# A decoder layer's output projection as seven products of 2x2 blocks, with W's block sums made by accumulating DMA

## The chip, the cores and the metric

One core of a Trainium2 chip runs the whole program. The metric is the device time of one execution in microseconds (us). Most executions of this kernel agree within 0.3%.

## The reference

The input x has 512 rows of 1024 channels. The layer computes h = RMSNorm(x) and one wide projection of h, which gives q, k, v and a gate path z for two attention branches (8 heads of 64 each) and two merge gates. Branch a is block-sparse softmax attention with a relative bias, branch b is stick-breaking attention. The end of the layer, where the change lies, is:

```python
ya = (merge_heads(oa) * jax.nn.silu(za)) @ w_up_moba[l]        # 512x512 @ 512x1024
yb = (merge_heads(ob) * jax.nn.silu(zb)) @ w_up_sb[l]
y = jax.nn.sigmoid(gl_a + gb[:D_MODEL]) * ya + jax.nn.sigmoid(gl_b + gb[D_MODEL:]) * yb
x = x + y @ w_out[l]                                            # 512x1024 @ 1024x1024
```

All of it is float32.

## The kernel before

**Precision.** Every large product is made of three matmuls of the float32r type (`mm3`, lines 144 to 147): each operand is split into a high part (a ScalarE copy that rounds) and a low part (VectorE subtracts the high part), and high x low, low x high and high x high are added in PSUM.

**Weights.** The host lays all weights out as chunks of 128 x 1024 in the order of use. `load_w` keeps three chunks ahead: `fetch_w` loads a chunk into a `wr` buffer (line 98, SyncE's queue, SP), ScalarE makes `wh` (line 107) and VectorE `wl` (line 109). There are three buffers of each.

**Order of the work.** The four projections qa, ka, va, vb come first. Then a loop over eight pairs of heads (four of branch a, four of branch b): the scores of both heads (six PSUM banks with the tag "s"), for each head softmax or stick-breaking, a transpose on VectorE (`turned`), a store to DRAM and a load back (`put`, `get`), the split of P (`split_p`), and `finish` for the pair before it: the product with V (`po`, line 418, one "s" bank) and its gate. Between these steps the list `FILLS` puts other projections, one chunk each, that keep TensorE (PE) fed: z, the merge gates g:0 to g:15, q and k of branch b, and `up("a", c)`. Each takes a bank with the tag "pj", of which there are two. Entry 4m + 2 of the list is the one between the two `finish` calls of pair m (26 is g:9, 30 is g:12). `up(br, c)` makes two tiles of y: PE sums the four blocks of 128 channels of one branch into a "pj" bank, VectorE multiplies it with the gate (line 476) and, for branch b, adds branch a's part (478) and splits y into `yh` (481) and `yl` (482). After the loop come `up("b", 0)` to `up("b", 3)`, then the output projection: for each half m of the columns, four row tiles of 128, eight k blocks, four chunks of W, each chunk used by 24 matmuls; the last row tile of the second half is cut into two of 256 columns. VectorE adds x to each bank (line 559) and SP stores it (560).

A scheduler in the compiler fixes the order of each engine's queue. It takes what it holds to be ready, earliest in the program first, so an instruction can stand in the queue ahead of others that come before it in the program. Buffers are handed out from pools by tag; an instruction that takes a buffer waits until the last reader of its former tenant is done.

Of the kernel before, what the change touches and what calls it, by code (L numbers as in the profile page):

```python
# [10 lines left out]
F32 = mybir.dt.float32  # L11
F32R = mybir.dt.float32r
BF16 = mybir.dt.bfloat16
AF = mybir.ActivationFunctionType
ALU = mybir.AluOpType
AX = mybir.AxisListType

P = 128
S = 512
D = 1024  # L20
KT = D // P
NT = S // P
H = 8
# [4 lines left out]
BIG = 1e30  # L28
TW = S + P
SM = 32  # L30
WARM = 8
BLK = [0, 4, 7, 9, 10]
PQ = BLK[-1] * 32


FILLS = ("za:0", "za:1", "za:2", "",
# [11 lines left out]
def hybrid_layer(ctx: ExitStack, tc: tile.TileContext, x, xT, w, rel, out):  # L48
    nc = tc.nc
    V, A, G, T = nc.vector, nc.scalar, nc.gpsimd, nc.tensor  # L50
# [3 lines left out]
    wp = ctx.enter_context(tc.tile_pool(name="wp", bufs=3))  # L54
    xp = ctx.enter_context(tc.tile_pool(name="xp", bufs=8))
    vp = ctx.enter_context(tc.tile_pool(name="vp", bufs=8))
# [7 lines left out]
    def bank(tag, name):  # L64
        return pp.tile([P, S], F32, tag=tag, bufs=BANKS[tag], name=name)

    def slot(name, dt=F32):
        return gp.tile([P, S], dt, tag="g", name=name)


    warm = tp.tile([P, S], BF16, tag="sx", bufs=2, name="warm")
    V.memset(warm, 0.0)
    half = cp.tile([P, NT], F32, name="half")
    G.memset(half, -0.5)
    spare = cp.tile([P, NT], F32, name="spare")
    A.activation(spare, half, AF.Copy)
    x0 = cp.tile([P, SM + S], F32, name="x0")
    sm = x0[:, :SM]
    nw, mb, qw, kw = sm[:, 0:8], sm[:, 8:24], sm[:, 24:25], sm[:, 25:26]


    ahead, low = [], {}
    count = [0]

    def load_w():

        while len(ahead) < 3 and count[0] < w.shape[0]:
            ahead.append(fetch_w(count[0]))
            count[0] += 1
        return ahead.pop(0)  # L90

    def fetch_w(c):
        raw = wp.tile([P, 1024], F32, tag="wr", bufs=3, name=f"wr{c}")
        cuts = ((0, 512), (512, 1024)) if c == 0 else ((0, 1024),)
        for a, b in cuts:
            if 0 < c < 4:
                raw_x(2 * c)
            nc.sync.dma_start(raw[:, a:b], w[c][:, a:b])
            if a == 0 and c < 4:
                for k in (0, 1) if c == 0 else (2 * c + 1,):  # L100
                    raw_x(k)
        hi = wp.tile([P, 1024], F32R, tag="wh", name=f"wh{c}")
        lo = wp.tile([P, 1024], F32R, tag="wl", name=f"wl{c}")
        if c == 0:
            low[c] = load_x(0)
        for a, b in cuts:
            A.activation(hi[:, a:b], raw[:, a:b], AF.Copy)  # L107
            with tc.issue_after(low[0]) if c == 0 else nullcontext():
                low[c] = V.tensor_tensor(lo[:, a:b], raw[:, a:b], hi[:, a:b].bitcast(F32), op=ALU.subtract).ins  # L109
        return hi, lo  # L110
# [6 lines left out]
    def raw_x(k):  # L117
        if k == 0:
            xraw[k] = x0[:, SM:]
            nc.sync.dma_start(x0, xT[:, :SM + S])  # L120
        else:
            xraw[k] = slot(f"xr{k}")
            nc.sync.dma_start(xraw[k], xT[:, SM + k * S:SM + (k + 1) * S])
# [17 lines left out]

    GROUPS = (("pj", "pj", "s", "s"), ("s", "s", "s", "s"))

    def mm3(ps, aH, aL, bH, bL, start, stop):
        T.matmul(ps, aH, bL, start=start, stop=False)  # L145
        T.matmul(ps, aL, bH, start=False, stop=False)  # L146
        T.matmul(ps, aH, bH, start=False, stop=stop)  # L147

    def section_tc(group, name, first=False, hooks=None):
        ps = [bank(GROUPS[group][t], f"{name}{t}") for t in range(NT)]  # L150
# [24 lines left out]
    def steps(c, n=NT):  # L175

        if c == 3:
            return [(kk, i) for i in range(n) for kk in range(2)]
        return [(kk, i) for kk in range(2) for i in range(n)]
# [3 lines left out]
    r = cp.tile([P, NT], F32, name="r")  # L183

    def row_norm():
# [5 lines left out]
        G.tensor_tensor(r, ss[:, 0, :], ss[:, 1, :], op=ALU.add)  # L191
        G.tensor_scalar(r, r, 1.0 / D, EPS, op0=ALU.mult, op1=ALU.add)
        G.tensor_tensor(r, r, half, op=ALU.pow)
# [98 lines left out]
    st, rows, last, qa, ka = {}, {}, {}, [], []  # L292
# [29 lines left out]
    v_of["b"] = split_v(ps_vb, "vb", [1.0] * NT)  # L322


    def chunk_ct(name):
        hi, lo = load_w()
        ps = bank("pj", name)
        for k in range(KT):
            ks = slice(k * P, (k + 1) * P)
            mm3(ps, hi[:, ks], lo[:, ks], xH[k], xL[k], k == 0, k == KT - 1)  # L330
        return ps
# [58 lines left out]
    def put(br, h):  # L390
        dr = dp.tile([P, 4 * PQ], F32, tag="pd", bufs=4, name=f"pd{br}{h}")
        for a in range(4):
            nc.sync.dma_start(bass.AP(tensor=dr.tensor, offset=dr.offset + a * PQ,
                                      ap=[[4 * PQ, 32], [32 * 4 * PQ, 4], [1, PQ]]),
                              turned[a * 32:(a + 1) * 32].rearrange("c q k r -> c q (k r)"))
        return dr

    def get(br, h, dr):
        pt = tp.tile([P, 4 * PQ], F32R, tag="pt", bufs=3, name=f"pt{br}{h}")
        nc.scalar.dma_start(pt.bitcast(F32), dr)  # L400
        return pt

    def split_p(br, h, pt):
        hi = tp.tile([P, 4 * PQ], F32R, tag="th", bufs=2, name=f"th{br}{h}")
        A.activation(hi, pt.bitcast(F32), AF.Copy)  # L405
# [37 lines left out]
    gates = {}  # L443
# [19 lines left out]


    yH, yL = [], []

    def up(br, c):
        hi, lo = load_w()
        for u in range(2):
            n = 2 * c + u  # L470
            ps = bank("pj", f"y{br}{n}")
            for p in range(4):
                ks = slice((u * 4 + p) * P, (u * 4 + p + 1) * P)
                mm3(ps, hi[:, ks], lo[:, ks], oH[br, p], oL[br, p], p == 0, p == 3)
            g = gates[n if br == "a" else 8 + n]
            V.tensor_tensor(g, ps, g, op=ALU.mult)  # L476
            if br == "b":
                V.tensor_tensor(g, g, gates[n], op=ALU.add)
                h = xp.tile([P, S], F32R, tag="xh", name=f"yh{n}")
                l = xp.tile([P, S], F32R, tag="xl", name=f"yl{n}")  # L480
                A.activation(h, g, AF.Copy)
                V.tensor_tensor(l, g, h.bitcast(F32), op=ALU.subtract)
                yH.append(h)
                yL.append(l)


    make = {"za": lambda i: f_z("a", i), "zb": lambda i: f_z("b", i), "q": f_q, "k": f_k, "g": f_g,
            "up": lambda i: up("a", i)}
    fills = [[(kind, int(i)) for kind, i in (word.split(":") for word in part.split())] for part in FILLS]

    def fill():
        for kind, i in fills.pop(0):
            make[kind](i)

# [14 lines left out]
    for m, (br, p) in enumerate(PAIRS):  # L509
        q, k = (qa, ka) if br == "a" else (qb, kb)  # L510
        sc, rw = {h: [None] * NT for h in (2 * p, 2 * p + 1)}, {h: [None] * NT for h in (2 * p, 2 * p + 1)}
        scores(br, p, q, k, sc)
        for b in range(2):
            h = 2 * p + b
            bias = load_bias(h) if br == "a" else None
            (softmax if br == "a" else stick)(h, sc[h], rw[h], bias, (3, 2, 1, 0))
            turn(br, h, rw[h])
            done[m, b] = put(br, h)
            fill()
            if not b:  # L520
                done[m, 0] = get(*head(m, 0), done[m, 0])
        for b in range(2):
            if m:
                finish(m - 1, b)
            if not b:
                done[m, 1] = get(*head(m, 1), done[m, 1])
            done[m, b] = split_p(*head(m, b), done[m, b])
            fill()
    fill()
    finish(len(PAIRS) - 1, 0)  # L530
    fill()
    finish(len(PAIRS) - 1, 1)
    fill()
    assert not fills

    for c in range(4):
        up("b", c)

    for m in range(2):
        ms = slice(m * S, (m + 1) * S)  # L540
        res = []
        for t in range(NT):
            xr = slot(f"xres{m}{t}")
            nc.sync.dma_start(xr, x[t * P:(t + 1) * P, ms])
            res.append(xr)
        parts = [(t, 0, S) for t in range(NT)]
        if m == 1:
            parts[3:] = [(3, 0, S // 2), (3, S // 2, S)]
        ps = [bank((GROUPS[1 - m] + ("s",))[i], f"out{m}{i}") for i in range(len(parts))]
        for c in range(4):  # L550
            hi, lo = load_w()
            for kk, i in steps(c, len(parts)):
                t, a, b = parts[i]
                k = 2 * c + kk
                ts = slice(t * P, (t + 1) * P)
                cs = slice(kk * S + a, kk * S + b)
                mm3(ps[i][:, :b - a], yH[k][:, ts], yL[k][:, ts], hi[:, cs], lo[:, cs], k == 0, k == KT - 1)
        for i, (t, a, b) in enumerate(parts):
            V.tensor_tensor(res[t][:, a:b], ps[i][:, :b - a], res[t][:, a:b], op=ALU.add)
            nc.sync.dma_start(out[t * P:(t + 1) * P, m * S + a:m * S + b], res[t][:, a:b])  # L560


def _t5_runs():
# [67 lines left out]
```

## Time and profile before

| | |
|---|---|
| median of 3 runs | 406.7 us (406.35 to 407.4) |
| the profiled execution | 407.05 us, of which the profile's span is 405.2 us |
| PE (matmuls) busy | 396.9 us, 98% of the span |
| VectorE (DVE) busy | 287.7 us, 71% |
| ScalarE (ACT) busy | 213.4 us, 53% |
| GpSimd (POOL) busy | 33.9 us, 8% |

Times in the rows are counted in us from the span's start. A row of a group of instructions names the line, engine, operation, written and read tiles, the shape and the count, and behind the bar the busy time, the mean duration of one in ns, and the idle time of the engine before them with what ended it. In a timeline the first two numbers are start and duration; brackets hold the idle time before the instruction and what ended it. Matmuls overlap, so their price is read from start to start.

### The profile page before, as it was taken

What the parts mean: (1) busy time and instruction counts of PE and PEld (TensorE: products, weight loads), DVE (VectorE), ACT (ScalarE), POOL (GpSimd) and SP (SyncE); (2) the same over time, 40 slices, a digit from 0 to 9 for tenths busy, and PEclk for the clock granted to TensorE, in tenths of its full rate; (3) what the DMA queues carried; (4) which work ended last, traced back from release to release, by engine and by line L of the source; (5) the groups of instructions that cost most, each with busy time, mean ns of one, the idle gap of its engine ahead of it and who ended that gap; (6) DMA issues with size and microseconds to landing.
All of it is one profiled execution on the core that took longest, in us unless ns stands there. A gap on an engine that the chain in (4) does not pass through costs nothing.

```text
span 405.2 us, 5404 instructions
## 1 busy us (share of the span) xinstructions
PE 396.9 (98%) x1920; PEld 328.0 (81%) x1920; DVE 287.7 (71%) x524; ACT 213.4 (53%) x353; POOL 33.9 (8%) x76
## 2 busy tenths in 40 slices
PE   8999999999999999999999999998998999999996
PEld 4788888887888888888888888886887888888885
DVE  4832759939788786888799599698589456862412
ACT  4772144646777879696763663563392454331110
POOL 2029953000000000000000000000000000000000
PEclk9999999999999999999999999999999999999999
DMA  8954277141677675756528537537526547433202
GB/s 264 356 212 133 79 235 258 66 142 52 171 220 222 213 237 167 213 180 228 175 68 246 171 104 231 172 97 228 168 80 194 163 135 246 146 105 104 104 2 104
DMA packets 28283, 67.77 MB, mean 167 GB/s; under 512 B 3288, under 2 KB 11736, under 8 KB 28256
## 3 DMA queue, kind: packets, MB, share of 16 engines
q1 hardware_dynamic: 24800, 54.84, 42.8%
q10 hardware_dynamic: 3456, 12.58, 9.8%
q8 instruction: 15, 0.25, 0.2%
q14 instruction: 12, 0.10, 0.1%
HBM read 54.81 MB, written 12.61 MB: 166 GB/s over the span
## 4 chain that ended last, share of the span: by engine, by line
PE 87%; DVE 5%; DMA 3%; ACT 2%; issue 1%; SPq 1%; DVEq 0%; ACTq 0%
PE gl L145 7%; PE gl L147 6%; PE gl L146 6%; PE out L146 4%; PE out L145 4%; PE out L147 4%; PE poa L418 2%; PE sa L345 2%; DVE sx L373 2%; PE za L145 2%; PE kb L145 2%; PE zb L145 2%; PE qb L145 2%; PE kb L147 2%; PE qb L147 2%; PE vb L147 2%
## 5 line engine op out<-in xcount | busy, mean ns | idle before, releaser
L109 DVE TENSOR_TENSOR wl<-wr,wh 128x1024 fp32r<-128x1024 f32 (+1 forms) x65 | 78.5, 1208 | 51.4 <-ACT wh L107 51.1
L107 ACT ACTIVATE wh<-wr 128x1024 fp32r<-128x1024 f32 (+1 forms) x65 | 67.8, 1043 | 60.6 <-PE out L147 20.5
L145 PE MATMUL gl<-xl,wh 128*128 128x512 f32 x128 | 51.0, 398 | 3.1 <-DVE gl L476 3.1
L146 PE MATMUL gl<-xh,wl 128*128 128x512 f32 x128 | 49.9, 390 | 0.0
L147 PE MATMUL gl<-xh,wh 128*128 128x512 f32 x128 | 49.9, 390 | 0.0
L145 PEld LDWEIGHTS gl<-xl,wh 128*128 128x128 f32 x128 | 24.0, 188 | 8.3 <-DVE gl L476 3.4
L147 PEld LDWEIGHTS gl<-xh,wh 128*128 128x128 f32 x128 | 24.0, 188 | 5.2
L146 PEld LDWEIGHTS gl<-xh,wl 128*128 128x128 f32 x128 | 24.1, 188 | 4.6
L146 PE MATMUL out<-wh,yl 128*128 128x512 f32 (+1 forms) x72 | 26.4, 366 | 0.0
L145 PE MATMUL out<-wl,yh 128*128 128x512 f32 (+1 forms) x72 | 26.4, 366 | 0.0
L147 PE MATMUL out<-wh,yh 128*128 128x512 f32 (+1 forms) x72 | 26.3, 365 | 0.0
L373 DVE TENSOR_TENSOR_SCAN sx<-om,begin 128x512 f32<-128x512 f32 (+3 forms) x32 | 24.6, 807 | 0.7 <-ACT om L369 0.7
L357 ACT ACTIVATE pa<-pa,m 128x512 f32<-128x512 f32 (+3 forms) x32 | 17.8, 558 | 6.4 <-DVE m L355 5.9
L405 ACT ACTIVATE thb<-ptb 128x1280 fp32r<-128x1280 f32 x8 | 10.2, 1273 | 15.2 <-DMA ptb<-pdb 15.2
L369 ACT ACTIVATE om<-sb 128x512 f32<-128x512 f32 (+3 forms) x32 | 14.8, 469 | 3.0 <-DVE sx L373 3.0
L448 ACT ACTIVATE gl<-gl,x 128x512 f32<-128x512 f32 x16 | 11.1, 695 | 9.9 <-PE gl L147 9.7
L406 DVE TENSOR_TENSOR ptb<-ptb,thb 128x1280 fp32r<-128x1280 f32 x8 | 11.9, 1482 | 5.7 <-ACT thb L405 5.7
L145 PEld LDWEIGHTS out<-wl,yh 128*128 128x128 f32 x72 | 13.6, 189 | 2.3
L147 PEld LDWEIGHTS out<-wh,yh 128*128 128x128 f32 x72 | 13.6, 188 | 2.2
L146 PEld LDWEIGHTS out<-wh,yl 128*128 128x128 f32 x72 | 13.6, 189 | 2.2
L355 DVE CUSTOM_DVE_ANT_0 pa<-sa,om 128x512 f32<-128x512 f32 (+3 forms) x32 | 14.9, 477 | 0.4 <-PE sa L345 0.3
L387 DVE STREAM_TRANSPOSE turned<-pa 128x256 f32<-128x256 f32 (+1 forms) x48 | 15.1, 367 | 0.0
(239 smaller groups left out, 975.5 us busy)
## 6 DMA issues: line engine op xcount, KB each, us to landing
wr<-in_w SPq DMA_DIRECT2D x63, 512.0 KB, 4.3
pda<-turned SPq DMA_DIRECT2D x32, 160.0 KB, 2.9
pta<-pda ACTq DMA_DIRECT2D x8, 640.0 KB, 3.9
pdb<-turned SPq DMA_DIRECT2D x32, 160.0 KB, 2.9
ptb<-pdb ACTq DMA_DIRECT2D x8, 640.0 KB, 3.9
xn<-in_x SPq DMA_DIRECT2D x8, 256.0 KB, 4.8
xs<-in_xT ACTq DMA_DIRECT2D x8, 256.0 KB, 3.1
om<-e_dr SPq DMA_DIRECT2D x8, 256.0 KB, 3.8
```

Of the source, the lines that this page charges most:

```text
L107: A.activation(hi[:, a:b], raw[:, a:b], AF.Copy)
L109: low[c] = V.tensor_tensor(lo[:, a:b], raw[:, a:b], hi[:, a:b].bitcast(F32), op=ALU.subtract).ins
L145: T.matmul(ps, aH, bL, start=start, stop=False)
L146: T.matmul(ps, aL, bH, start=False, stop=False)
L147: T.matmul(ps, aH, bH, start=False, stop=stop)
L355: V.tensor_tensor_reduce(p, sc[i], bias[:, S - n:], scale=1.0, scalar=3e38, op0=ALU.add, op1=ALU.min, accum_out=m[:, 0:1])
L357: A.activation(p, p, AF.Exp, bias=m[:, 0:1], scale=-1.0, accum_out=m[:, 1:2])
L369: A.activation(om[:, e - 1 - n:e - 1], z, AF.Sigmoid, scale=-1.0)
L373: V.tensor_tensor_scan(sx[:, n - 1::-1] if n == S else sx[:, :n][:, ::-1], om[:, e - n:][:, ::-1], begin[:, S - n:][:, ::-1], 0.0, op0=ALU ...
L387: V.transpose(turned[:, :, at:at + (n - 1) * step + 1:step, :].rearrange("p q j r -> p j q r"), rows[i][:, j * P:(j + n) * P].rearrange("p ...
L406: V.tensor_tensor(pt, pt.bitcast(F32), hi.bitcast(F32), op=ALU.subtract)
L448: A.activation(g, ps, AF.Sigmoid, bias=mb[:, i:i + 1])
```

## The change

The output projection y @ W (512 x 1024 by 1024 x 1024) is cut into 2x2 blocks: y into row halves of 256 and channel halves of 512, W into 512 x 512 blocks named 11, 21, 12, 22. Instead of eight block products it makes seven: A11 with 11, A12 with 21, S2 with T2, S1 with T1, S3 with T3, S4 with 22, A22 with T4. T1 = 11 + 12, T2 = 22 + T1, T3 = 22 + 12, T4 = 21 + T2. Each T is made in SBUF by a plain load and an accumulating DMA issued by GpSimd, two halves each, in buffers of the V tiles ("v"): T1 and T2 after pairs 4 and 5, T3 and T4 in `up("b", 2)` and `up("b", 3)`. S1 = A21 - A22, S2 = S1 - A11, S3 = A11 - A21 and S4 = A12 + S2 are made by VectorE from y (`sums_21`, `sum_4`). Partial results are kept in PSUM banks X, Y and Z: X takes A11 11, then S2 T2, then S3 T3, then A22 T4, and is read between them. x is added by a load ahead for two of the four blocks of the output and by an accumulating DMA (`store`) for the other two. W's chunks hold the same data as before; 14 of them are used in place of 8, each by 12 matmuls.

Apart from that, the fills 6, 10, 14, 18, 22, 26 and g:14 and the first six tiles of `up("b")` take an "s" bank in place of a "pj" bank.

```diff
+TERMS = {1: ("11", "12"), 2: ("22", "T1"), 3: ("22", "12"), 4: ("21", "T2")}
+BLOCKS = [b + h for b in ("11", "21", "12", "22") for h in "ab"]
+OUT = [b + h for b in ("11", "21", "T2", "T1", "T3", "22", "T4") for h in "ab"]
+SUMS = {4: 1, 5: 2}
...
+    def sum_w(i):
+
+        for half in "ab":
+            t = vp.tile([P, H // 2, 2, P], F32, tag="v", name=f"T{i}{half}").rearrange("p a b d -> p (a b d)")
+            for n, blk in enumerate(TERMS[i]):
+                src = sums[blk + half] if blk[0] == "T" else w[WO + BLOCKS.index(blk + half)]
+                if n == 0:
+                    nc.sync.dma_start(t, src)
+                else:
+                    nc.gpsimd.dma_start(t, src, accum_op=ALU.add)
+            sums[f"T{i}{half}"] = t
...
-        raw = wp.tile([P, 1024], F32, tag="wr", bufs=3, name=f"wr{c}")
...
+        if c >= WO and OUT[c - WO][0] == "T":
+            raw = sums[OUT[c - WO]]
+        else:
+            raw = wp.tile([P, 1024], F32, tag="wr", bufs=3, name=f"wr{c}")
...
-        ps = bank("pj", name)
+        ps = bank(home[0], name)
...
-            ps = bank("pj", f"y{br}{n}")
+            ps = bank(home[0] if br == "a" or n > 5 else "s", f"y{br}{n}")
...
-                h = xp.tile([P, S], F32R, tag="xh", name=f"yh{n}")
-                l = xp.tile([P, S], F32R, tag="xl", name=f"yl{n}")
-                A.activation(h, g, AF.Copy)
-                V.tensor_tensor(l, g, h.bitcast(F32), op=ALU.subtract)
-                yH.append(h)
-                yL.append(l)
+                split_y(n)
+
+    def split_y(n):
+        g = gates[8 + n]
+        yH.append(xp.tile([P, S], F32R, tag="xh", name=f"yh{n}"))
+        yL.append(xp.tile([P, S], F32R, tag="xl", name=f"yl{n}"))
+        part(yH[n], yL[n], g, slice(0, HS))
+
+    def part(hi, lo, raw, cs, at=None):
+
+        at = at or cs
+        A.activation(hi[:, at], raw[:, cs], AF.Copy)
+        V.tensor_tensor(lo[:, at], raw[:, cs], hi[:, at].bitcast(F32), op=ALU.subtract)
+
+    def sums_21(k):
+
+        d, a, b = gates[k], gates[8 + k], gates[12 + k]
+        V.tensor_tensor(d[:, :HS], a[:, :HS], a[:, HS:], op=ALU.subtract)
+        V.tensor_tensor(a[:, HS:], a[:, HS:], b[:, HS:], op=ALU.subtract)
+        V.tensor_tensor(a[:, :HS], a[:, HS:], a[:, :HS], op=ALU.subtract)
+        sH.append(slot(f"sh{k}", F32R))
+        sL.append(slot(f"sl{k}", F32R))
+        part(sH[k], sL[k], a, slice(0, S))
+
+    def sum_4(k):
+
+        a, b = gates[8 + k], gates[12 + k]
+        V.tensor_tensor(b[:, :HS], b[:, :HS], a[:, :HS], op=ALU.add)
+        part(yH[k], yL[k], b, slice(0, HS), slice(HS, S))
+
+    def split_3(k):
+        t = slot(f"s3{k}", F32R)
+        s3.append((t[:, :HS], t[:, HS:]))
+        part(*s3[k], gates[k], slice(0, HS))
...
-    def fill():
+    def fill(tag="pj"):
+
+        home[0] = tag
         for kind, i in fills.pop(0):
             make[kind](i)
...
             done[m, b] = split_p(*head(m, b), done[m, b])
-            fill()
+            fill("pj" if b or not fills[1] else "s")
+        if m in SUMS:
+            sum_w(SUMS[m])
     fill()
     finish(len(PAIRS) - 1, 0)
-    fill()
+    fill("s")
     finish(len(PAIRS) - 1, 1)
     fill()
...
     for c in range(4):
         up("b", c)
+        if c > 1:
+            sum_w(c + 1)
...
+    def product(ps, a, start):
+        for c in range(2):
+            hi, lo = load_w()
+            for kk, t in ([(kk, t) for kk in range(2) for t in range(2)] if c == 0 else
+                          [(kk, t) for t in range(2) for kk in range(2)]):
+                k = 2 * c + kk
+                ts, cs = slice(t * P, (t + 1) * P), slice(kk * S, (kk + 1) * S)
+                mm3(ps[t], a[k][0][:, ts], a[k][1][:, ts], hi[:, cs], lo[:, cs], start and k == 0, k == 3, True)
...
+    def residual(r, c):
         res = []
+        for t in range(2):
+            res.append(slot(f"xres{r}{c}{t}"))
+            nc.sync.dma_start(res[t], x[rows_of(r, c, t)])
+        return res
+
+    def store(res, r, c, late=True):
+
+        for t in range(2):
+            ts, ms = rows_of(r, c, t)
+            if late:
+                nc.gpsimd.dma_start(res[t], x[ts, ms], accum_op=ALU.add)
+            nc.sync.dma_start(out[ts, ms], res[t])
+
+    def take(ps, name):
+        res = [slot(f"{name}{t}") for t in range(2)]
+        for t in range(2):
+            A.activation(res[t], ps[t], AF.Copy)
+        return res
...
+    X, Z = ([bank("s", f"{n}{t}") for t in range(2)] for n in ("ox", "oz"))
+    product(X, A11, True)
+    for k in range(4):
+        sums_21(k)
+        if k == 1:
+            r11 = take(X, "r11")
+    S1 = [(sH[k][:, right], sL[k][:, right]) for k in range(4)]
+    S2 = [(sH[k][:, left], sL[k][:, left]) for k in range(4)]
+    product(Z, A12, True)
+    add(r11, Z, r11)
+    store(r11, 0, 0)
+    r12 = residual(0, 1)
+    product(X, S2, False)
+    for k in range(4):
+        split_3(k)
+    add(r12, r12, X, ALU.subtract)
+    Y = [bank("s", f"oy{t}") for t in range(2)]
+    product(Y, S1, True)
+    r22 = take(Y, "r22")
+    for k in range(4):
+        sum_4(k)
+    product(X, s3, False)
+    for k in range(4, KT):
+        part(yH[k], yL[k], gates[8 + k], right)
+    add(r22, r22, X, ALU.subtract)
+    store(r22, 1, 1)
+    r21 = residual(1, 0)
+    V.tensor_tensor(r21[1][:, right], X[1][:, right], r21[1][:, right], op=ALU.add)
+    product(Y, S4, False)
+    add(r12, Y, r12)
+    store(r12, 0, 1, False)
+    last = bank("pj", "last")
+    parts = ((0, X[0], 0, S), (1, X[1], 0, HS), (1, last, HS, S))
+    for c in range(2):
+        hi, lo = load_w()
+        for t, ps, a, b in parts:
+            for kk in range(2):
                 k = 2 * c + kk
...
+                ts, cs = slice(t * P, (t + 1) * P), slice(kk * S + a, kk * S + b)
+                mm3(ps[:, :b - a], A22[k][0][:, ts], A22[k][1][:, ts], hi[:, cs], lo[:, cs], ps is last and k == 0,
+                    k == 3, True)
+            if c:
+                V.tensor_tensor(r21[t][:, a:b], ps[:, :b - a], r21[t][:, a:b], op=ALU.add)
+                nc.sync.dma_start(out[(2 + t) * P:(3 + t) * P, a:b], r21[t][:, a:b])
```

## Rows read from the trace of the kernel before

**Rows 1.** The page's busy time, share of the span and instructions of each engine.
```profile
PE 396.9 (98%) x1920; PEld 328.0 (81%) x1920; DVE 287.7 (71%) x524; ACT 213.4 (53%) x353; POOL 33.9 (8%) x76
```

**Rows 2.** The page's chain of work that ended last, by engine.
```profile
PE 87%; DVE 5%; DMA 3%; ACT 2%; issue 1%; SPq 1%; DVEq 0%; ACTq 0%
```

**Rows 3.** The longest of PE's waits over the whole span: who waited for whom, us in total, times, longest.
```profile
PE gl L145 <- DVE gl L476: 3.1, 2, 1.9
```

**Rows 4.** Windows: pairs 5 and 6 of the loop, `up("b")`, and the output projection. Columns: length, busy us (and instructions) of PE, PE's weight loads, DVE, ACT, POOL, then PE's granted clock, DMA share, GB/s.
```profile
228.34:261.20 32.86, 32.86 (x167) 27.35 (x168) 28.30 (x46) 18.14 (x32) 0.00 (x0) 1.00 0.55 165
261.20:294.90 33.70, 31.79 (x158) 26.36 (x156) 26.47 (x45) 16.61 (x30) 0.00 (x0) 1.00 0.51 156
...
335.86:357.84 21.98, 21.98 (x98) 18.20 (x97) 17.47 (x24) 8.51 (x11) 0.00 (x0) 1.00 0.56 180
357.84:401.95 44.11, 44.11 (x217) 37.22 (x215) 14.85 (x19) 7.52 (x8) 0.00 (x0) 1.00 0.21 73
```

**Rows 5.** Timeline of PE in the output projection: the first matmul, the first of the next three, the first after eight triples (a chunk), and the last two, of 256 columns.
```profile
357.84 0.39 PE L145 MATMUL out<-wl,yh 128*128 128x512 f32 x1
358.52 0.39 PE L145 MATMUL out<-wl,yh 128*128 128x512 f32 x1
...
363.28 0.39 PE L145 MATMUL out<-wl,yh 128*128 128x512 f32 x1
...
401.55 0.28 PE L146 MATMUL out<-wh,yl 128*128 128x256 f32 x1
401.67 0.28 PE L147 MATMUL out<-wh,yh 128*128 128x256 f32 x1
```

**Rows 6.** Timelines around bank waits: in pair 6, the split of g:9's weights, the last read of the pair's scores, then DVE, PE's product with V and g:9's first matmul; in pair 7, g:12's first matmul.
```profile
263.13 1.22 DVE L109 TENSOR_TENSOR wl<-wr,wh 128x1024 fp32r<-128x1024 f32 x1
268.79 0.38 ACT L371 ACTIVATE pb<-sb 128x128 f32<-128x128 f32 x1
270.47 2.04 DVE L373 TENSOR_TENSOR_SCAN sx<-om,begin 128x512 f32<-128x512 f32 x2
274.07 0.80 PE L418 MATMUL pob<-ptb,vbs 128*128 128x512 f32 x4
276.04 1.29 DVE L476 TENSOR_TENSOR gl<-ya,gl 128x512 f32<-128x512 f32 x2
276.78 0.50 PE L145 MATMUL gl<-xl,wh 128*128 128x512 f32 x1 [1.91 <-DVE gl L476]
...
310.29 0.50 PE L145 MATMUL gl<-xl,wh 128*128 128x512 f32 x1 [1.22 <-DVE gl L476]
```

**Rows 7.** Groups by line and shape: the splits of W's chunks, of y, additions over PSUM, and a 256-column operation on DVE; below, one split of W by ACT in the output stage.
```profile
L109 DVE TENSOR_TENSOR wl<-wr,wh 128x1024 fp32r<-128x1024 f32 x63 | 77.1, 1224 | 50.6 <-ACT wh L107 50.3
L482 DVE TENSOR_TENSOR yl<-gl,yh 128x512 fp32r<-128x512 f32 x8 | 5.5, 690 | 2.3 <-ACT yh L481 2.1
L559 DVE TENSOR_TENSOR xres<-out,xres 128x512 f32<-128x512 f32 x7 | 4.7, 689 | 12.8 <-PE out L147 12.8
L375 DVE TENSOR_TENSOR pb<-pb,sx 128x256 f32<-128x256 f32 x8 | 3.3, 408 | 0.0
L107 ACT ACTIVATE wh<-wr 128x1024 fp32r<-128x1024 f32 x63 | 66.5, 1056 | 58.0 <-PE out L147 20.5 <-PE ka L147 12.2 <-PE ya L147 7.6
...
363.53 1.06 ACT L107 ACTIVATE wh<-wr 128x1024 fp32r<-128x1024 f32 x1 [2.93 <-PE out L147]
```

**Rows 8.** Timeline of DVE: two products of 256 columns and what comes after them, and a stretch of `up("b")`.
```profile
274.38 0.61 DVE L375 TENSOR_TENSOR pb<-pb,sx 128x256 f32<-128x256 f32 x2
...
343.26 1.22 DVE L109 TENSOR_TENSOR wl<-wr,wh 128x1024 fp32r<-128x1024 f32 x1
344.40 0.68 DVE L482 TENSOR_TENSOR yl<-gl,yh 128x512 fp32r<-128x512 f32 x1
345.00 0.68 DVE L476 TENSOR_TENSOR gl<-yb,gl 128x512 f32<-128x512 f32 x1
...
350.06 0.68 DVE L476 TENSOR_TENSOR gl<-yb,gl 128x512 f32<-128x512 f32 x1
350.84 0.69 DVE L482 TENSOR_TENSOR yl<-gl,yh 128x512 fp32r<-128x512 f32 x1
```

**Rows 9.** DMA issues: destination and source, queue, count, size of one, median us from issue to landing.
```profile
wr<-in_w SPq DMA_DIRECT2D x63, 512.0 KB, 4.3
xres<-in_x SPq DMA_DIRECT2D x8, 256.0 KB, 5.0
xr<-in_xT SPq DMA_DIRECT2D x7, 256.0 KB, 6.5
out_y<-xres SPq DMA_DIRECT2D x7, 256.0 KB, 2.0
```

**Rows 10.** Timelines: the last products with V of branch a and of branch b on PE (each followed by four matmuls more, 0.58 us later), and SP's loads of x for the output.
```profile
216.07 0.74 PE L418 MATMUL poa<-tha,vas 128*128 128x512 f32 x4
329.34 0.74 PE L418 MATMUL pob<-thb,vbs 128*128 128x512 f32 x4
332.88 1.80 SPq L544 DMA_DIRECT2D xres<-in_x  x4
```

**Rows 11.** Timeline of the end, on SP and DVE.
```profile
401.73 1.05 SPq L560 DMA_DIRECT2D out_y<-xres  x2
401.99 0.42 DVE L559 TENSOR_TENSOR xres<-out,xres 128x256 f32<-128x256 f32 x1 [0.29 <-PE out L147]
```

More of the change, by code (lines that the diff above doesn't have):

```diff
@@ L19 @@
 S = 512
+HS = S // 2
 D = 1024
@@ L79, in hybrid_layer @@
     nw, mb, qw, kw = sm[:, 0:8], sm[:, 8:24], sm[:, 24:25], sm[:, 25:26]
-    ahead, low = [], {}
+    ahead, low, sums = [], {}, {}
+    WO = w.shape[0] - len(BLOCKS)
+    def sum_w(i):
[8 more added lines that the diff above has]
+            sums[f"T{i}{half}"] = t
     count = [0]
     def load_w():
-        while len(ahead) < 3 and count[0] < w.shape[0]:
+        while len(ahead) < 3 and count[0] < len(OUT) + WO:
             ahead.append(fetch_w(count[0]))
@@ L92, in fetch_w @@
     def fetch_w(c):
-        raw = wp.tile([P, 1024], F32, tag="wr", bufs=3, name=f"wr{c}")
         cuts = ((0, 512), (512, 1024)) if c == 0 else ((0, 1024),)
[L95 to L101, printed above, removed]
+        if c >= WO and OUT[c - WO][0] == "T":
+            raw = sums[OUT[c - WO]]
+        else:
+            raw = wp.tile([P, 1024], F32, tag="wr", bufs=3, name=f"wr{c}")
+            for a, b in cuts:
+                if 0 < c < 4:
+                    raw_x(2 * c)
+                nc.sync.dma_start(raw[:, a:b], w[c if c < WO else WO + BLOCKS.index(OUT[c - WO])][:, a:b])
+                if a == 0 and c < 4:
+                    for k in (0, 1) if c == 0 else (2 * c + 1,):
+                        raw_x(k)
         hi = wp.tile([P, 1024], F32R, tag="wh", name=f"wh{c}")
@@ L142, in hybrid_layer, with mm3 @@
     GROUPS = (("pj", "pj", "s", "s"), ("s", "s", "s", "s"))
[L144 to L147, printed above, removed]
+    def mm3(ps, aH, aL, bH, bL, start, stop, on=False):
+        T.matmul(ps, aH, bL, start=start, stop=False, skip_group_check=on)
+        T.matmul(ps, aL, bH, start=False, stop=False, skip_group_check=on)
+        T.matmul(ps, aH, bH, start=False, stop=stop, skip_group_check=on)
     def section_tc(group, name, first=False, hooks=None):
@@ L322, in hybrid_layer @@
     v_of["b"] = split_v(ps_vb, "vb", [1.0] * NT)
+    home = ["pj"]
     def chunk_ct(name):
         hi, lo = load_w()
-        ps = bank("pj", name)
+        ps = bank(home[0], name)
         for k in range(KT):
@@ L465, in hybrid_layer @@
     yH, yL = [], []
+    sH, sL, s3 = [], [], []
     def up(br, c):
@@ L537, in hybrid_layer @@
         up("b", c)
-    for m in range(2):
-        ms = slice(m * S, (m + 1) * S)
-        res = []
[L542 to L553, printed above, removed]
-                k = 2 * c + kk
[L555 to L560, printed above, removed]
+        if c > 1:
+            sum_w(c + 1)
@@ new lines, in hybrid_layer @@
+    left, right = slice(0, HS), slice(HS, S)
+    A11 = [(yH[k][:, left], yL[k][:, left]) for k in range(4)]
+    A12 = [(yH[k + 4][:, left], yL[k + 4][:, left]) for k in range(4)]
+    A22 = [(yH[k + 4][:, right], yL[k + 4][:, right]) for k in range(4)]
+    S4 = [(yH[k][:, right], yL[k][:, right]) for k in range(4)]
+    def product(ps, a, start):
[6 more added lines that the diff above has]
+                mm3(ps[t], a[k][0][:, ts], a[k][1][:, ts], hi[:, cs], lo[:, cs], start and k == 0, k == 3, True)
@@ new lines, in rows_of @@
+    def rows_of(r, c, t):
+        return slice((2 * r + t) * P, (2 * r + t + 1) * P), slice(c * S, (c + 1) * S)
+    def residual(r, c):
+        res = []
+        for t in range(2):
[8 more added lines that the diff above has]
+            nc.sync.dma_start(out[ts, ms], res[t])
@@ new lines, in take, with add @@
+    def take(ps, name):
[3 more added lines that the diff above has]
+        return res
+    def add(res, a, b, op=ALU.add):
+        for t in range(2):
+            V.tensor_tensor(res[t], a[t], b[t], op=op)
+    X, Z = ([bank("s", f"{n}{t}") for t in range(2)] for n in ("ox", "oz"))
[4 more added lines that the diff above has]
+            r11 = take(X, "r11")
```

## The prediction

> **What bounds the kernel now.** I read the page's busy table first: TensorE is busy 396.9 of 405.2 us, VectorE 71%, ScalarE 53%, GpSimd 8% [rows 1]. A busy PE can still hide waits, so next the chain that ended last: 87% of it is PE [rows 2]. PE's own waits are short: the largest sum is 3.1 us, in two places, where a projection ("gl") waits for VectorE to empty a bank (line 476) [rows 3]. So time comes off only if PE gets less to do, or if those two waits go; anything moved to another engine is free until it makes PE wait. Then the stage windows [rows 4]: in the output projection (357.84 to 401.95) PE is busy 44.11 of 44.11 us and VectorE only 14.85; in the stage before it, up("b") (335.86 to 357.84), VectorE is busy 17.47 of 21.98. TensorE's granted clock is 1.00 (2.4 GHz) in all of them, so one price per matmul holds.
>
> **The matmuls.** In the output stage three matmuls of 512 columns start 0.68 us after the three before, so 0.2267 us each; 256 columns cost 0.12 [rows 5]. The durations of the same rows (0.39, 0.28) overlap and are not prices. Before: 2 column halves x 8 k x 4 row tiles x 3 = 192, of which one row tile of the second half is cut in two: 168 x 0.2267 + 48 x 0.12 = 43.85 us; the trace has 401.79 - 357.84 = 43.95, so the price is right. After: seven products of 4 k x 2 row tiles x 3 = 24, 168 in all, with 12 of the last cut in two: 156 x 0.2267 + 24 x 0.12 = 38.25. **-5.6 us.** The Trainium skill (TensorE: Matmul & The Clock Gate, "Wait — 56ns, not 53.3ns?") gives a warm matmul N/2.4 GHz plus 2.5 ns from start to start, 215.8 ns for 512 and 109.2 for 256. By it the edit would bring an estimated 12 x 0.2158 + 24 x 0.1092 = 5.2 us; the rows here are 5% dearer, and I go by the rows.
>
> **The banks.** The chunk g:9 (fill 26) should have started when PE left pob, at 274.87, but began at 276.78: its "pj" bank was waiting for line 476 of up("a"), which VectorE reached only after scans and what followed them [rows 6]. Its weights had been split at 264.4. After the change this fill takes an "s" bank. All six score banks of that pair had been read by ScalarE at 269.17, so one is free. **-1.9 us.** The other wait (1.22 us at 310.29) is g:12, whose next fill is empty, so it keeps "pj"; I count nothing. The other fills that go to "s" had no wait to lose [rows 3]; they start, like g:9, after a product with V, when the pair's scores have been read, so I count no new one.
>
> **What is added, and its cover.** Call T0 the start of the output stage. PE wants products at T0, then each 5.44 us: A11, A12, S2 (T0+10.9), S1 (16.3), S3 (21.8), S4 (27.2), A22 (32.6).
>
> *W's splits.* A chunk of 1024 columns now feeds 12 matmuls instead of 24, so 14 chunks instead of 8 pass ScalarE (1.056) and VectorE (1.224), one per 2.72 us [rows 7]. A chunk's buffer is freed two chunks ahead, ScalarE starts 0.25 after that [rows 5, 7], so a split takes 2.6 of 5.44 us: 2.9 us of slack for whatever stands in front of it.
>
> *y's sums.* On VectorE: 12 subtractions and 4 additions of 256 columns (0.408), 4 splits of 512 (0.690), 12 more of 256 (the second half of y is no longer split in up("b"), which gives back 8 x 0.28 = 2.3 us there), 8 additions or subtractions of 512 over PSUM (0.689) and a few small ones. From start to start VectorE is quicker than its durations: 512 columns 0.60, 1024 columns 1.14, 256 columns 0.26 to 0.33 [rows 8]. After T0 that makes 12 x 1.14 + 28 x 0.33 + 4 x 0.60 + 8 x 0.60 + 1.3 at the end + about 2 left of up("b") = 33.4 of 38.25 us, 87%; with the durations, 100%. VectorE's idle 4.5 us in up("b") [rows 4] and the 2.3 given back take some of it earlier, since its queue is not in the program's order (lines 476 and 482 pass each other [rows 8]). The tight place is S2: before T0+14.3 (its fourth k) VectorE owes 2 left over, four splits (4.6), the S sums (4 x 1.6 = 6.3) and two additions (1.2), 14.1 us, less what it did before T0. S0 and S1 can run there, as y4 and y5 are ready by T0-3. I take 0, with 3 us of margin at best and none at worst: bounds 0 and 3.6 (below).
>
> *W's sums by DMA.* Eight accumulating DMAs of 512 KB and eight plain loads for the sums; of the 14 chunks six are loaded directly, where eight were. No accumulating DMA, and none from GpSimd, is in this trace. Nearest rows: a plain 512 KB load lands after 4.3 us, 256 KB after 2.0 (store), 5.0 and 6.5 (loads) [rows 9]. An accumulate reads two streams and writes one, so I put it, as an estimate, between 1 and 2 loads: 4.3 to 8.6 us. T1 and T2 take the buffers of va, free at 217.3 after the last poa [rows 10], 149 us before T2 is wanted; T3 and T4 take those of vb, free at 330.5, 27 us before T0, and are wanted at about T0+16.5 to T0+30. Four of 8.6, one after another behind a load, end at T0+12. Cost 0. SP's queue ran loads this early before, too (x's rows at 332.88, over 40 us ahead of use [rows 10]), and GpSimd has no other work in these windows [rows 4]. T1 and T2 move about 4 to 6 MB in the stretch 217 to 290 us, in which the 16 DMA engines are busy 0.51 to 0.55 of the time [rows 4]. Their neighbours on SP, the stores of P, feed a product one pair (33 us) later.
>
> *The end.* The last addition is again one of 256 columns, and the stretch from the last matmul's end to the span's end (3.4 us) stays [rows 11]. C22 is subtracted at T0+27.2+1.5 = T0+28.7, gets x by an accumulating DMA, and is then stored (2.0). The span ends at T0+41.65; as the final store shares SP's queue, x must have landed by about T0+38.6: 9.9 us of room against 5.0 to 8.6. Cost 0.
>
> **Sum.** -5.6 - 1.9 = -7.5 us. The profiled execution took 407.05 (span 405.2), so 399.55; the median of the runs shown is 406.7, 0.35 under it: **399.2 us**.
>
> **Rivals.**
> 1. *VectorE late for S2 (or S4, T3).* For: 87% load, a fixed queue order, ScalarE and VectorE alternating in each split (VectorE waits 2.1 us for the eight of y [rows 7], 0.70 where it has nothing else). Against: 6.8 us free before T0. Worst order: all four S in front of T2's split. From y7 ready (an estimate: T0 + 0.2 + 4 steps of 0.69 = T0+2.9), 4 x (1.6+0.7) = 9.2, the split of 21b (1.14) and that of T2's first half (1.22) end at T0+14.5, 3.6 us after need. 1.5 to 3.6 lost: 400.7 to 402.8.
> 2. *The bank wait moves.* PE reaches the next thing that waits on VectorE 1.9 us sooner and waits there. For: VectorE is busy 26.5 of 33.7 us in that pair and has lag behind scans [rows 4, 6]. Against: it idles 7 us per pair. 401.1.
> 3. *The second wait goes as well* (other bank order): 398.0.
> 4. *The other side: C22's and W's accumulating DMAs are slow.* Place: the store at the end, on SP's queue. From 9.9 us issue-to-landing it costs one for one; from 9.9 + 7.5 = 17.4 us the kernel is no faster, from 18.6 slower by over 0.3%. At twice the dearest row, 13 us, the end moves by 3.1: 402.3; at 20 us, 409. W's T4 becomes late only past 13 us each. Against: all rows of that size are at 6.5 or less. [...]
>
> **Chances.** Forecast 0.46 (own range 398.4 to 400.4), rival 1 0.22, rival 2 0.13, rival 3 0.08, rival 4 0.11, of which 0.07 slower than before. The measurement tells 0.3% (1.2 us) from no change. Faster 0.89, same 0.04, slower 0.07. The range goes from rival 3 (398.0, less 0.2) to rival 1's worst with some of rival 2: 397.8 to 404.0.
>
> **What would show it.** Output stage 38.3 us long from its first to its last matmul; no PE wait near 275 but one of about 1.2 near 308; VectorE near 30 us busy in the output stage; accumulating DMAs landing in 5 to 9 us; the last DMA the store of C21. The forecast is wrong if PE shows idle time in front of S2's or T2's matmuls, or if the span ends on a store of C22.

## The result and the profile after

Six executions of the changed kernel took 400.2 to 408.09 us, median 406.14, beside 407.04 (406.35 to 407.67) of the kernel before. The ratio of after to before is 0.9886, 95% interval 0.9844 to 0.9929, so about 402.4 us. The ratios here and below leave out executions that lie over 1.5% above the fastest of their kernel, here three (406.49, 407.72 and 408.09). All three have a mean granted clock under 1.00 (0.996 and twice 0.991), as has the profiled one (0.990), so the median is nearer to what the kernel usually takes. Faster, as forecast, but by 4.6 us at the ratio and by 0.9 at the medians, where 7.5 was forecast. And the executions now spread over 8 us. Those of the kernel before don't spread so far, but they don't agree within 0.3% either: the 54 that were taken beside the experiments below run from 405.47 to 410.23.

The page of the execution profiled after (405.8 us, span 404.0): busy time, share and instructions of each engine, TensorE's granted clock in 40 slices, and the chain that ended last.

```profile
PE 392.7 (97%) x1884; PEld 324.3 (80%) x1884; DVE 305.3 (76%) x565; ACT 225.8 (56%) x379; POOL 44.6 (11%) x88
...
PEclk9999999999999999999999999889999999999999
...
PE 84%; DVE 6%; DMA 5%; ACT 2%; issue 1%; SPq 1%; DVEq 0%; ACTq 0%
```

Against [rows 1, 2], PE has 4 us less to do, yet the span is only 1.2 us shorter, DMA's share of the chain has grown from 3 to 5%, and two slices (near 252 to 273 us) have a lower clock. PE's waits, in us in total, times and longest:

```profile
PE ya L172 <- DVE kb3l L305: 5.0, 1, 5.0
PE gl L172 <- DVE gl L506: 1.2, 1, 1.2
```

Of the two waits in [rows 3] the one of 1.9 is gone and the one of 1.2 stays, as forecast. New is a single wait of 5.0 us in front of `up("a")`, in pair 5. The last two windows of this view (columns as in [rows 4]) are the stages the change was aimed at, the ones before them the pair with the wait:

```profile
230.00:238.00 8.00, 8.00 (x37) 6.67 (x36) 7.99 (x15) 7.11 (x19) 0.40 (x1) 1.00 1.05 278
238.00:250.00 12.00, 12.00 (x59) 10.15 (x59) 9.73 (x18) 3.01 (x5) 1.35 (x2) 1.00 1.01 242
250.00:262.00 12.00, 7.35 (x33) 5.75 (x31) 6.75 (x12) 4.94 (x7) 0.00 (x0) 0.89 0.51 167
264.00:266.00 2.00, 2.00 (x7) 1.52 (x6) 0.16 (x1) 0.09 (x1) 0.00 (x0) 0.50 0.73 225
...
340.30:362.30 22.00, 22.00 (x98) 18.23 (x98) 19.24 (x33) 8.80 (x16) 2.42 (x3) 1.00 0.88 231
362.30:400.60 38.30, 38.30 (x181) 32.12 (x180) 30.87 (x51) 19.71 (x30) 3.54 (x4) 1.00 0.43 115
```

The output stage is 38.3 us long and PE never waits in it. The trouble lies 100 us earlier: from 230 to 250 us the DMA engines are fully busy (1.05 and 1.01; the kernel before has 0.20 and 0.65 there):

```profile
230.00:238.00 8.00, 8.00 (x43) 6.64 (x40) 7.96 (x13) 7.11 (x19) 0.00 (x0) 1.00 0.20 67
238.00:250.00 12.00, 12.00 (x59) 10.19 (x58) 11.74 (x24) 4.75 (x7) 0.00 (x0) 1.00 0.65 185
```

What fills them are T1 and T2. Issues of these in the kernel after, with us from issue to landing:

```profile
T1a<-in_w POOLq DMA_DIRECT2D x1, 512.0 KB, 9.2
T2a<-in_w SPq DMA_DIRECT2D x1, 512.0 KB, 11.2
T1b<-in_w POOLq DMA_DIRECT2D x1, 512.0 KB, 11.5
T2b<-in_w SPq DMA_DIRECT2D x1, 512.0 KB, 8.9
T2a<-T1a POOLq DMA_DIRECT2D x1, 512.0 KB, 5.1
T2b<-T1b POOLq DMA_DIRECT2D x1, 512.0 KB, 8.3
```

The chain through this place, in order of time (start, duration, what), shows how a full DMA system becomes a wait of PE:

```profile
240.72 8.54 DMA pdb<-turned
...
249.29 5.52 DMA ptb<-pdb
...
254.83 1.28 ACT thb L434
...
256.14 1.49 DVE ptb L435
...
257.66 0.69 DVE ob L456
...
258.38 1.23 DVE wl L135
...
261.63 0.70 DVE kb3l L305
...
262.38 0.80 PE ya L172
263.17 0.43 PE ya L173
```

The last store of the first head's P lands after 8.54 us; 2.2 to 3.6 was the range of these stores in the same stretch before. The load back (`ptb`) stands in ScalarE's queue and waits for it. ScalarE and VectorE work their queues in order, so they stand still too, as a timeline shows (brackets: idle before, and what ended it):

```profile
249.66 0.60 ACT L304 ACTIVATE qb3h<-qb 128x512 fp32r<-128x512 f32 x1 [6.31 <-DMA pdb<-turned]
254.83 1.27 ACT L434 ACTIVATE thb<-ptb 128x1280 fp32r<-128x1280 f32 x1 [4.57 <-DMA ptb<-pdb]
256.14 1.49 DVE L435 TENSOR_TENSOR ptb<-ptb,thb 128x1280 fp32r<-128x1280 f32 x1 [4.46 <-ACT thb L434]
```

Before, the same three had 4.58 us of idle time (for q:3's products), none, and 0.41. `thb` starts at 254.83, where it was 248.85 before, so 6 us late. Behind it in VectorE's queue is `kb3l` (line 305), the last read of the "pj" bank in which k:3 was made, and the second tile of `up("a", 0)` takes that bank. The first tile's last matmul starts at 256.96; the second's first is this:

```profile
262.38 0.80 PE L172 MATMUL ya<-ola,wh 128*128 128x512 f32 x1 [5.03 <-DVE kb3l L305]
```

So this wait, too, is one for a bank, like the two of the kernel before. PE idles 5.03 us, and TensorE's clock falls to 0.50 (1.2 GHz): the nine matmuls from 262.38 to 266.2 start 0.43 us apart instead of 0.2267, 1.8 us lost. The sum closes within 0.1: the first output matmul is at 362.34 against 357.84 [rows 5], +4.5, and 5.0 + 1.8 less the 1.9 of the wait that is gone and 0.3 of an earlier start is 4.6; the output stage gives 5.65 back; 4.5 - 5.65 = -1.15, and the spans differ by -1.2.

### The profile page after: what moved, and what is told of

Its sections match the earlier page's. It is cut to its first block, busy times and chain, and to the rows that moved or that the text cites. A ratio compares the mean times of both kernels' runs of the same rounds, so it can differ in the third digit from the quotient of the medians.

```text
span 404.0 us, 5458 instructions
## 1 busy us (share of the span) xinstructions
PE 392.7 (97%) x1884; PEld 324.3 (80%) x1884; DVE 305.3 (76%) x565; ACT 225.8 (56%) x379; POOL 44.6 (11%) x88
## 4 chain that ended last, share of the span: by engine, by line
PE 84%; DVE 6%; DMA 5%; ACT 2%; issue 1%; SPq 1%; DVEq 0%; ACTq 0%
PE gl L172 7%; PE gl L174 6%; PE gl L173 6%; PE poa L447 2%; DMA pdb<-turned 2%; PE sa L374 2%; PE za L172 2%; PE za L173 2%; PE za L174 2%; PE vb L173 2%; PE vb L172 2%; PE vb L174 2%; PE ka L173 2%; PE yb L174 2%; PE va L174 2%; PE va L173 2%
## 5 line engine op out<-in xcount | busy, mean ns | idle before, releaser
L135 DVE TENSOR_TENSOR wl<-wr,wh 128x1024 fp32r<-128x1024 f32 (+1 forms) x63 | 76.1, 1208 | 33.5 <-ACT wh L133 28.7
L133 ACT ACTIVATE wh<-wr 128x1024 fp32r<-128x1024 f32 (+1 forms) x63 | 65.7, 1043 | 43.4 <-PE ka L174 12.2
L103 POOL DMA_DIRECT2D T1a<-in_w x1 | 1.1, 1090 | 161.0 <-DMA T1a<-in_w 161.0
L172 PE MATMUL ya<-ola,wh 128*128 128x512 f32 x32 | 13.4, 419 | 5.0 <-DVE kb3l L305 5.0
L398 ACT ACTIVATE om<-sb 128x512 f32<-128x512 f32 (+3 forms) x32 | 14.8, 470 | 3.5 <-DVE sx L402 3.4
L416 DVE STREAM_TRANSPOSE turned<-pb 128x256 f32<-128x256 f32 (+1 forms) x48 | 14.7, 363 | 2.4 <-DMA pdb<-turned 2.3
L400 ACT ACTIVATE pb<-sb 128x512 f32<-128x512 f32 (+3 forms) x32 | 15.0, 482 | 0.0
L435 DVE TENSOR_TENSOR pta<-pta,tha 128x1280 fp32r<-128x1280 f32 x8 | 11.8, 1473 | 3.5 <-ACT tha L434 3.5
L404 DVE TENSOR_TENSOR pb<-pb,sx 128x512 f32<-128x512 f32 (+3 forms) x32 | 14.2, 477 | 0.1
```

The lines of the kernel that those rows point to most:

```text
L172: T.matmul(ps, aH, bL, start=start, stop=False, skip_group_check=on)
L398: A.activation(om[:, e - 1 - n:e - 1], z, AF.Sigmoid, scale=-1.0)
L400: A.activation(p, z, AF.Sigmoid)
L416: V.transpose(turned[:, :, at:at + (n - 1) * step + 1:step, :].rearrange("p q j r -> p j q r"), rows[i][:, j * P:(j + n) * P].rearrange("p ...
L435: V.tensor_tensor(pt, pt.bitcast(F32), hi.bitcast(F32), op=ALU.subtract)
```

## The experiments

My theory after the result: products and banks give what was forecast, and T1's and T2's transfers take part of it back through the stores of P. Rivals: the score banks cause the new wait (rival 2), or VectorE's new work does. Medians are in us; the kernel before, on the same chips, had medians of 408.38 (for e1 to e4), 407.51 (e0, e5, e6, e7) and 407.92 (e8, e9).

| kernel | median (lowest to highest, runs) | ratio to before, 95% |
|---|---|---|
| e0: the changed kernel again | 405.97 (401.22 to 407.52, 9) | 0.9924 [0.9886, 0.9963] |
| e1: before, banks alone | 404.91 (404.73 to 406.27, 7) | 0.9921 [0.9894, 0.9949] |
| e2: after without the sums of W | 401.38 (399.62 to 402.06, 6) | 0.9814 [0.978, 0.9849] |
| e3: T1, T2 behind the last store of P | 406.76 (404.94 to 407.93, 12) | 0.9959 [0.9935, 0.9983] |
| e4: before, T1 and T2 made, not used | 411.53 (408.06 to 414.89, 12) | 1.0064 [1.0032, 1.0096] |
| e5: plain copies for the accumulates | 399.0 (398.88 to 399.42, 4) | 0.9787 [0.9755, 0.9819] |
| e6: half a sum per pair | 400.01 (398.84 to 401.94, 6) | 0.9816 [0.9782, 0.9851] |
| e7: e6, and g:12 in a score bank | 399.28 (398.39 to 399.89, 5) | 0.979 [0.9761, 0.982] |
| e8: e6 without the bank part | 403.81 (402.14 to 406.02, 7) | 0.9897 [0.9858, 0.9936] |
| e9: only T2 moved | 399.51 (398.46 to 400.46, 6) | 0.9806 [0.9765, 0.9847] |

**e1: the bank part alone**, put into the kernel before.

```diff
-            ps = bank("pj", f"y{br}{n}")
+            ps = bank(home[0] if br == "a" or n > 5 else "s", f"y{br}{n}")
...
-            fill()
+            fill("pj" if b or not fills[1] else "s")
```

> The kernel before with the bank part of the change alone: the fills 6, 10, 14, 18, 22, 26 and g:14 and six tiles of up("b") take an "s" bank; the output projection stays eight block products. If the 1.9 us wait before g:9 was only a matter of its bank, 1.9 us less than before (405.1 where before takes 407.0) and no PE wait near 275. If the time only moves to the next wait (my rival 2), within 0.5 us of before. If the bank rotation is what makes PE wait 5 us in front of up:0 in the changed kernel, that wait shows here and the time is 2 to 4 us more than before.

The wait of 1.9 is gone, none of 5 us appears (one line is left beside the start's), and the span is 402.9, 2.3 less. So the new choice of banks doesn't make the new wait: rival 2 falls.

```profile
PE gl L145 <- DVE gl L478: 1.2, 1, 1.2
```

**e2: no sums of W.** The chunks of T1 to T4 are plain loads of the sum's first block.

```diff
-        if c >= WO and OUT[c - WO][0] == "T":
-            raw = sums[OUT[c - WO]]
-        else:
+        if True:
...
-        if m in SUMS:
-            sum_w(SUMS[m])
```

> The changed kernel without W's sums: each T chunk is a plain load of its first block, so the output is not the layer's; nothing accumulates into W, T1 and T2 are not in SBUF while the pairs run. Theory A (the transfers of T1 and T2 beside pair 5 hold up the stores of P, then ScalarE's queue, then PE): no 5 us wait, 7.5 us less than before in every execution (399.5 where before takes 407.0) with a spread under 1.5 us. Rival B (the banks, or another order of the queues, make the wait): the wait stays and the time is 405 to 408 in some executions, as in the changed kernel.

-1.86%, 7.6 us, with no wait in front of `up("a")`. VectorE's new work is all in this kernel, so that work is not the cause either.

**e4: the transfers alone.** The kernel before makes T1 and T2 in pairs 4 and 5, with the same queues, and uses neither.

```diff
+        if m in (4, 5):
+            sum_w(m - 3)
```

> The kernel before with the transfers of T1 and T2 alone (four plain loads, four accumulating DMAs, issued where the changed kernel issues them; nobody reads the sums). Theory A: PE waits near 255 to 262 us that the kernel before has not, 2 to 7 us in some or all executions, with a spread of several us: 408 to 414 where before takes 407.0. Rival B: as before within 0.5 us.

Slower by 0.64%, 2.6 us, and the wait is there, in a kernel whose products are untouched. The clock falls here too, about 1.3 us after PE has resumed at 259.72:

```profile
PE gl L162 <- DVE gl L493: 2.3, 2, 1.2
PE ya L162 <- DVE kb3l L295: 2.0, 1, 2.0
...
260.00:262.00 2.00, 2.00 (x8) 1.59 (x8) 1.51 (x2) 0.00 (x0) 0.00 (x0) 0.76 0.66 253
262.00:264.00 2.00, 2.00 (x5) 1.10 (x4) 0.00 (x0) 0.59 (x1) 0.00 (x0) 0.50 0.76 265
```

With e2, which has neither these transfers nor the wait, this shows that the transfers are the cause.

**e3: T1 and T2 later**, their loads on SP behind the last store of P, and so their accumulates after it.

```diff
-                    nc.sync.dma_start(t, src)
+                    with tc.issue_after(puts[-1]):
+                        nc.sync.dma_start(t, src)
...
+    sum_w(1)
+    sum_w(2)
```

> The changed kernel with T1 and T2 made later: their loads stand on SP's queue behind the last store of P, so all four sums are made between about 315 and 370 us. Theory A: as without the sums, 399 to 400 in every execution, if T2 is there by T0+8; each us that T2 is late is lost in front of S2 (T1, T2, T3 and T4, 8.8 to 11.2 us each and partly side by side, from 318 on: T2's second half by about 350, T0 = 354, so no loss). Rival B: the wait in front of up:0 stays, 405 or more in some executions.

A miss. The wait at `up("a")` is gone, and another has come: the last head's P had been stored, but its load back now shared the DMA engines with the sums and took 8.6 us (4.0 is the median of these loads), and no pair comes after it to fill PE's time.

```profile
PE pob L451 <- ACT thb L438: 3.4, 1, 3.4
```

So what matters is not the stores as such, but any store or load of P that the transfers meet.

**e0 and e5: is it the bytes or the accumulate?** e0 is the changed kernel once more. In e5 the eight accumulates of W are plain copies, from the same places to the same places on the same queue, so the sums are left out and nothing else.

```diff
-                    nc.gpsimd.dma_start(t, src, accum_op=ALU.add)
+                    nc.gpsimd.dma_start(t, src)
```

> The changed kernel once more, on the chip of the runs below. Theory A (T1's and T2's transfers beside pair 5 delay the stores of P): 0 to 7 us of waiting in front of up:0, so a spread of several us, about 400 to 408 where before takes 407. Rival C (the spread belongs to the chip of the first measurement): a spread as that of before.

> The changed kernel with the eight accumulating DMAs of W's sums as plain copies of the same size from the same queue (GpSimd's), so the sums and the output are wrong. If the bytes and their place beside the stores of P make the wait (theory A in its plain form): the wait in front of up:0 stays, 402 to 408. If it is the accumulate itself that is slow (8 to 11 us a piece in the changed kernel's trace against 4.3 us of a plain load): copies land in 4 to 6 us, the wait shrinks under 1 us, 399.5 to 401 with a spread under 2 us.

e0 repeats the result, spread included, with the wait at the same place:

```profile
PE ya L172 <- DVE kb3l L305: 3.1, 1, 3.1
```

e5 takes 399.0, the fastest of all, within 0.6 us over four runs, with no such wait. Its DMA share is 0.93 and 0.74 where it was 1.05 and 1.01. GpSimd's queue, packets, MB and share of the 16 engines' time, first after, then e5:

```profile
q0 software_dynamic: 1728, 5.24, 7.2%
```

```profile
q0 software_dynamic: 1728, 5.24, 4.3%
```

The same packets and bytes took 1.7 times as long. Both figures hold the four accumulates of x, which e5 doesn't change; e2 has only those on this queue (1.7% of 400.3 us). Without them W's eight transfers alone come to an estimated 2.2 times. It is the accumulate, not the bytes or the queue.

**e6 and e9: the sums moved apart.** e6 makes one half of T1 or T2 per pair, its load issued by ScalarE behind the pair's last `th`, the copy of P's high part; e9 leaves T1 where it was and moves only T2's halves.

```diff
-SUMS = {4: 1, 5: 2}
+SUMS = {4: (1, "a"), 5: (1, "b"), 6: (2, "a"), 7: (2, "b")}   # e6
+SUMS = {4: (1,), 6: (2, "a"), 7: (2, "b")}                     # e9
...
+                if n == 0 and after is not None:
+                    with tc.issue_after(after):
+                        nc.scalar.dma_start(t, src)
```

> The changed kernel with T1's and T2's halves one per pair (T1a in pair 4, T1b in 5, T2a in 6, T2b in 7), each load issued by ScalarE behind the copy that ends the pair's load of P, so one load and one accumulate fall into the stretch in which no store of P runs. Theory A: no wait of more than 1 us in front of up:0, 399.5 to 401 in nearly all executions, spread under 2 us. If any transfer of a sum near the pairs costs PE time, 402 to 406 again, with waits in pairs 5 to 7.

> The changed kernel with T1 made where it was (both halves after pair 4) and only T2's halves moved, one behind pair 6's last load of P and one behind pair 7's. If T1's two loads and two accumulates, 220 to 238 us, delay the stores of P by themselves: a wait of 1 to 4 us in front of up:0, 401 to 405 with spread. If it takes T2's four transfers on top of them (the stretch 238 to 250, where the trace of the changed kernel has the DMA engines at 1.01): no such wait, 399 to 400.5.

Both keep everything the change computes and reach the forecast: -1.84% and -1.94%, 7.5 and 7.9 us. Made one at a time, accumulates land in 5.0 to 5.4 us (e6, T1a, T1b, T2a). In e9 T1's two still took 7.9 and 9.8, and did no harm: from 230 us on the DMA share is below 1 again, and PE's one wait after the start is the old one.

```profile
238.00:250.00 12.00, 12.00 (x59) 10.17 (x58) 11.61 (x22) 4.71 (x8) 0.00 (x0) 1.00 0.70 203
...
PE gl L175 <- DVE gl L511: 1.3, 1, 1.3
```

So T2's four transfers on top of T1's, inside pair 5, are what tips it.

The profiled executions line up by the start of `thb` in pair 5. At 248.85 (before), 248.67 (e5), 249.86 (e6) and 248.06 (e9) PE doesn't wait; at 252.18 (e4), 253.49 (e0) and 254.83 (after) it waits 2.0, 3.1 and 5.0 us. Whether another bank for the second tile of `up("a", 0)` would have hidden the delay was not tested.

**e8: the products alone**, e6 with every tile back in "pj".

```diff
-            ps = bank(home[0] if br == "a" or n > 5 else "s", f"y{br}{n}")
+            ps = bank("pj", f"y{br}{n}")
...
-        home[0] = tag
+        home[0] = "pj"
```

> The run with one half of T1 and T2 per pair, without the bank part of the change: every fill and every tile of up takes a "pj" bank as in the kernel before. If the parts add up: the seven products alone bring 5.6 us (38.3 us of output stage in place of 43.9) and the two waits of 1.9 and 1.2 us in front of g:9 and g:12 are back, so 401.4 where before takes 407.0. If the bank part is needed for the seven products to pay (X, Y, Z and up("b") short of banks), more waits show and it is 403 or more.

-1.03%, 4.2 us. With e1's 0.79% (3.2 us) that makes 7.4, beside 7.5 in e6: the parts add up, within intervals of over 1 us each. Its span, 401.4, is 3.8 us under before's, but its start, which the change doesn't touch, took longer: the weight products of qa begin at 13.4 us (11.8 before). (This start varies from profile to profile; e7's is 13.1.) Without these 1.6 us it is 5.4, against the 5.6 forecast. The two bank waits are back:

```profile
PE gl L175 <- DVE gl L511: 3.1, 2, 2.1
```

**e7: the other bank wait.** e6 with g:12's fill in a score bank.

```diff
-            fill("pj" if b or not fills[1] else "s")
+            fill("s" if not b and m else "pj")
```

> As the run with one half per pair, and the fill g:12 takes an "s" bank as well. The wait of 1.2 us in front of it (in every trace so far) goes: 1.2 us less than that run. If that bank is then short elsewhere (scores or products with V of pair 7): no gain or up to 2 us more, and a PE wait on an "s" bank shows.

The wait of 1.2 is gone, and PE waits nowhere after the start. The median is 0.7 under e6's, but the intervals overlap, so a gain over e6 isn't established. At 0.979 of before, e7 beats both kernels.

## Why the prediction was right and wrong

**A figure inside the range, by luck.** The ratio's 402.4 lies within the stated 397.8 to 404.0. But the room above 399.2 was left for VectorE late at S2 and for a bank wait that moves (rivals 1 and 2), and neither came; the loss came from a step that was put at nothing. The median of all six executions, 406.14, lies above the range.

**Right.** The price per matmul: 38.25 us worked out, 38.3 measured. (The rule of the Trainium skill, TensorE: Matmul & The Clock Gate, "Wait — 56ns, not 53.3ns?", would make it an estimated 156 x 0.2158 + 24 x 0.1092 = 36.3; the rows decide for 0.2267 and 0.12. They are 5% dearer than the rule for 512 columns, as the prediction says, but 10% for 256.) The bank: 1.9 us gone and 1.22 left, now at 314.79. VectorE: 30.87 us busy in the output stage, where near 30 was forecast, and no wait at S2, so rival 1 did not come. The end: C22's accumulates landed in 4.5 us, against 9.9 of room, and the span ends 3.4 us after the last matmul, as before.

**Wrong: the step "W's sums by DMA. Cost 0".** It has two errors. The first is the sentence that the stores of P "feed a product one pair (33 us) later". That is the distance to the last reader, not to the first instruction that is held up. The load behind the stores stands in ScalarE's own queue, and `thb` behind it; both engines work in order, so everything after them is late at once, the last read of the bank for `up("a")` among it. The question that the prediction should have asked of its own line, what is queued behind the waiting instruction, was asked for SP and GpSimd only.

The second is the size. 4.3 to 8.6 us per accumulate fits one alone (5.0 to 5.4 in e6), but not several at once: 9.2 and 11.5 for T1's here, and 14.2 in e6 for T3's second half. The share of 0.51 to 0.55 that I read for this stretch [rows 4] is a mean over a pair; T1 and T2 together ran from 220 to 249 us, because the scheduler put T2's loads, which the program has behind pair 5, into SP's queue ahead of pair 5's stores.

Together these cost about 6.8 us in the profiled execution (5.0 of waiting and 1.8 of clock), and by the medians of kernels measured side by side 6.0 (e0 less e6) to 7.0 (e0 less e5). Rival 4 named the culprit, slow accumulates, and looked for it at the end of the kernel, where there was room.

**Why executions differ.** Of the 15 executions of the changed kernel (both runs), four had a mean granted clock of 0.999 or 1.0 and took 400.2 to 402.04; three with 0.996 took 404.0 to 406.49; eight with 0.990 or 0.991 took 405.38 to 408.09. So in about one of four the forecast nearly came true. What decides whether the wait grows isn't shown; with T2 moved, no execution out of twelve (e6, e9) falls below 0.999.

**A gain that I hadn't counted.** The banks were forecast at 1.9 us, 2.3 came in e1's trace, and 3.2 (2.1 to 4.3) by its ratio. A likely reason: 22 of 54 executions of the kernel before had a clock of 0.995 or 0.996, with a median of 409.3 against 407.2 for the other 32. None of e1's seven is below 0.998, while five of e8's seven, with the bank waits back, are at 0.994 to 0.996. That the clock falls behind the bank wait in those executions was not profiled. The wait of 2.0 in e4 shows that one of this length can do it, and e8's profile that it need not: its bank wait of 2.1 left the clock at 1.00.

## What to carry to other kernels

When work goes to DMA because its result is wanted late, look not at its own deadline but at the transfers it will meet: sum the bytes for the stretch in which the scheduler will really issue them, and look for a short store or load there that an in-order compute engine waits on. Make accumulates one at a time, behind the last such transfer of a stage that has cover after it (e6, e9); "as late as possible" (e3) only moved the wait to where no cover was left. And a wait of PE costs more than its length when the clock falls behind it.

## What the runs showed of the hardware

An accumulating DMA of 512 KB lands in 5.0 to 5.4 us when no other accumulate runs beside it (e6) and in up to 14.8 us beside others (e8, T3's second half); as a queue it occupied the DMA engines 1.7 times as long as plain copies of the same packets and bytes (after, e5). Why is open. After PE had idled 2.0, 3.1 or 5.0 us the granted clock fell to 0.50 (e4, e0, after), and in the profile after it came back at about 266.2, 3.8 us after PE had resumed. After the bank waits of 1.1 to 2.1 us in the profiles it stayed at 1.00. As e8's wait of 2.1 is longer than e4's of 2.0, the length of the wait alone doesn't decide; what does isn't shown.
